# Up-projection of a gated MLP by seven block products in place of eight

## The chip, the cores and the metric

One core of a Trainium2 chip runs the whole program. The metric is the time of one execution on the device in microseconds; the time of a kernel is the median of its runs.

## What is computed

Two layers of a streaming encoder over 576 token columns (512 of one group, 64 of another, which share all weights). A layer has token mixers, cross-attention and a gated MLP with a causal convolution of width 3 between up-projection and activation; each has a norm before it and one behind it:

```python
def conv_ffn(h, w_up, conv_w, w_down, prev):
    u, state = causal_dwconv(h @ w_up, conv_w, prev)
    a, g = u[..., :D_FF], u[..., D_FF:]
    return (jax.nn.gelu(a, approximate=True) * g) @ w_down, state
...
    c = cross_attention(rmsnorm(x, g[2]), mem_k, mem_v, lp['w_ca_q'], lp['w_ca_o'])
    x = x + rmsnorm(c, g[3])
    f, ffn_state = conv_ffn(rmsnorm(x, g[4]), lp['w_up'], lp['ffn_conv_w'], lp['w_down'], hist['ffn'])
    x = x + rmsnorm(f, g[5])
```

Here `D_MODEL` is 1024 and `D_FF` 2816; all inputs and results are float32.

## The kernel before

Features lie on the 128 partitions, tokens on the columns, in two halves of 288 (`HALF`). Every float32 operand of a matmul is split (`split`, L129): ACT copies it to a rounded high part, DVE subtracts that from the source and has the low part. A product of two such operands is three matmuls (`mm3`, L152: lines 155 to 157). `load_w` (L137) has SP load 1024 weight columns and splits them in two pieces of 512, `wh` and `wl`, of which ten stand at a time.

The MLP is `ffn` (L1200). The 44 up-projection tiles go in 22 pairs, one tile of the gelu side and one of the gate side. A tile has eight k steps, so a pair has, in `emit`, 2 tiles x 2 token halves x 8 k steps x 3 matmuls. `scaled` (L317) takes each result out of PSUM on DVE and multiplies it by the norm `rn` on the way, for the split activations `h` in `boundary` (L320) are not yet divided by it. `done` runs the convolution (`conv_taps`, L942: one ACT operation and two DVE operations a tile, "taps" below), gelu, the product of the halves (DVE, L1226 and L1227) and the split into `ah` and `al`. After every four or five pairs (`STAGES`) `down` multiplies what is there by its part of the down-projection and adds it to `m` (DVE, L1269); `NACT` such activation tiles stand at a time. The last stage goes through `out_proj` (L333), which finishes the first token half (squares, mean, norm, addition to `x`) beside the matmuls of the second. The two pairs ahead of all others ("early tiles", `FEARLY`) run half 0 of both pairs before half 1, so that the boundary of half 1, from cross-attention, may still be at work.

The engines' orders come from a scheduler that reorders the program: weights of the next pair stand between a pair's evacuations and taps. Each engine then keeps its order. Results go to four PSUM banks (`DENSE`) in turn.

## Time and profile before

| | us |
|---|---|
| median of three runs | 2536.48 |
| lowest and highest | 2530.51, 2537.34 |
| the profiled execution | 2537.41 |
| its span in the profile | 2535.3 |
| PE, DVE, ACT, POOL busy | 2418.0, 1576.6, 1143.4, 403.6 |

Busy time is the union of an engine's instructions. On PE a matmul's row shows some 0.3 us, but matmuls overlap; count and stretch together give what one takes. The granted clock of a stretch is a share of 2.4 GHz, so 0.50 is 1.2 GHz. On a row of the timeline, the time in brackets is idle time ahead of the instruction and what ended it.

### The profile page before, as it was taken

To read this page: it belongs to the slowest core of one execution; us is meant where nothing else is said; L and a number is where in the kernel's file an instruction comes from. 1 tells how busy PE (TensorE), PEld (TensorE's weight loads), DVE (VectorE), ACT (ScalarE), POOL (GpSimd) and SP (SyncE) were. 2 spreads that over 40 slices of the span, in tenths; PEclk is the share of its full clock that TensorE was granted. 3 is DMA by queue.
4 is the path that set the end of the run, shared out by engine and by line. 5 is a ranking of instruction groups with operands and counts; after the bars stand their busy time and mean duration, and the time that the engine had idled before them with its cause. 6 is when DMAs were issued, how large, how long until landed. Compare 5 with 4: busy or idle time off the path is not lost. (4 is left out here: it accounts for less than half of the span.)

```text
span 2535.3 us, 45273 instructions
## 1 busy us (share of the span) xinstructions
PE 2418.0 (95%) x17478; PEld 2320.8 (92%) x17478; DVE 1576.6 (62%) x3249; ACT 1143.4 (45%) x2479; POOL 403.6 (16%) x723
## 2 busy tenths in 40 slices
PE   6999999999999999999989999999999899999997
PEld 6888897899998899999987889889999889999997
DVE  7757768644436675566676677774453767566565
ACT  4556545533345543333345554553233564433332
POOL 4000021002221421011130001100121323101012
PEclk9999999999998899999988999999999999999998
DMA  6763143333222032322233223323233202222321
GB/s 226 233 188 98 59 134 100 113 102 102 84 98 90 28 101 63 101 71 84 78 98 103 96 71 108 121 89 122 88 103 113 87 23 87 86 90 62 93 84 52
DMA packets 97510, 249.10 MB, mean 98 GB/s; under 512 B 12520, under 2 KB 26920, under 8 KB 97104
## 3 DMA queue, kind: packets, MB, share of 16 engines
q1 hardware_dynamic: 88880, 230.67, 29.4%
q0 software_dynamic: 3296, 8.54, 1.2%
q10 hardware_dynamic: 5120, 7.00, 0.8%
q8 instruction: 138, 2.26, 0.4%
q14 instruction: 76, 0.62, 0.1%
HBM read 206.18 MB, written 30.94 MB: 94 GB/s over the span
## 5 line engine op out<-in xcount | busy, mean ns | idle before, releaser
L123 ACT ACTIVATE wh<-raw 128x512 fp32r<-128x512 f32 (+2 forms) x674 | 405.1, 612 | 663.3 <-PE ps_S L156 300.9
L126 DVE TENSOR_TENSOR wl<-raw,wh 128x512 fp32r<-128x512 f32 (+2 forms) x674 | 444.7, 668 | 251.8 <-ACT wh L123 239.6
L155 PE MATMUL ps_d<-hh,wh 128*128 128x288 f32 (+1 forms) x1672 | 503.9, 301 | 0.8 <-DVE qbd L135 0.5
L157 PE MATMUL ps_d<-hh,wl 128*128 128x288 f32 (+1 forms) x1672 | 503.1, 301 | 0.0
L156 PE MATMUL ps_d<-hl,wh 128*128 128x288 f32 (+1 forms) x1672 | 502.1, 300 | 0.0
L156 PE MATMUL ps_S<-hl,wh 128*128 128x288 f32 (+1 forms) x1256 | 372.7, 297 | 0.4 <-DVE hl L285 0.4
L155 PE MATMUL ps_S<-hh,wh 128*128 128x288 f32 (+1 forms) x1256 | 371.7, 296 | 1.2 <-ACT hh L123 1.2
L157 PE MATMUL ps_S<-hh,wl 128*128 128x288 f32 (+1 forms) x1256 | 371.7, 296 | 0.0
L155 PEld LDWEIGHTS ps_d<-hh,wh 128*128 128x128 f32 (+1 forms) x1672 | 319.2, 191 | 3.3 <-issue 1.4
L157 PEld LDWEIGHTS ps_d<-hh,wl 128*128 128x128 f32 (+1 forms) x1672 | 319.0, 191 | 1.6 <-DVE wl L126 0.3
L156 PEld LDWEIGHTS ps_d<-hl,wh 128*128 128x128 f32 (+1 forms) x1672 | 319.2, 191 | 1.3 <-issue 0.2
L155 PEld LDWEIGHTS ps_S<-hh,wh 128*128 128x128 f32 (+1 forms) x1256 | 235.5, 188 | 2.8 <-ACT hh L123 1.8
L156 PEld LDWEIGHTS ps_S<-hl,wh 128*128 128x128 f32 (+1 forms) x1256 | 235.5, 187 | 1.5 <-DVE hl L285 0.6
L157 PEld LDWEIGHTS ps_S<-hh,wl 128*128 128x128 f32 (+1 forms) x1256 | 235.1, 187 | 0.6
L1086 POOL TENSOR_TENSOR mf<-mf,tm 128x288 f32<-128x288 f32 x64 | 64.4, 1006 | 451.4 <-DVE tm L1085 451.4
L955 POOL COPY fst<-u 128x2 f32<-128x2 f32 x88 | 32.2, 366 | 472.6 <-DVE u L319 472.6
L155 PE MATMUL ps_S<-ah,wh 128*128 128x288 f32 x352 | 105.6, 301 | 0.4 <-DVE m L1257 0.4
L156 PE MATMUL ps_S<-al,wh 128*128 128x288 f32 x352 | 105.8, 301 | 0.0
L157 PE MATMUL ps_S<-ah,wl 128*128 128x288 f32 x352 | 105.1, 299 | 0.0
L155 PE MATMUL ps_d<-ah,wh 128*128 128x288 f32 x352 | 104.0, 295 | 1.0 <-ACT ah L123 0.9
L157 PE MATMUL ps_d<-ah,wl 128*128 128x288 f32 x352 | 103.9, 295 | 0.0
L156 PE MATMUL ps_d<-al,wh 128*128 128x288 f32 x352 | 103.9, 295 | 0.0
(500 smaller groups left out, 5810.5 us busy)
## 6 DMA issues: line engine op xcount, KB each, us to landing
raw<-in_w_dram SPq DMA_DIRECT2D x250, 512.0 KB
raw<-in_down_dram SPq DMA_DIRECT2D x48, 256.0 KB
raw<-in_down_dram SPq DMA_DIRECT2D x32, 320.0 KB
of<-o_scr SPq DMA_DIRECT2D x24, 288.0 KB
x<-in_xT_dram SPq DMA_DIRECT2D x16, 288.0 KB
o_scr<-of SPq DMA_DIRECT2D x16, 288.0 KB
raw<-in_ukv_dram SPq DMA_DIRECT2D x8, 512.0 KB
kc_scr<-k SPq DMA_DIRECT2D x8, 512.0 KB
```

The lines of the kernel that those rows point to most:

```text
L123: self.nc.scalar.activation(out, in_, func, scale=scale, **k)
L126: self.nc.vector.tensor_tensor(out, a, b, op=ALU.subtract)
L155: mm(ps, w[0], x[0], start=first, stop=False)
L156: mm(ps, w[0], x[1], start=False, stop=False)
L157: mm(ps, w[1], x[0], start=False, stop=last)
L955: self.nc.gpsimd.tensor_copy(dst[:, 0:2], u[:, 512:514])
L1086: nc.gpsimd.tensor_tensor(mf[j][:, a:b], mf[j][:, a:b], tm[:, a:b], op=ALU.add)
```

## The change

Pairs 2 to 21 of the up-projection are computed by Strassen's scheme: the k range and the tokens are halved, and the two weight tiles of a pair, gelu side `a` and gate side `g`, are the two block rows. Seven products of four k steps, of sums of weights (`weights`, POOL) with sums of tokens (`token_sums`, once a layer), take the place of eight, and DVE adds up the results as it takes them out of PSUM (`pair`). The early pairs 0 and 1 stay as they are. So that tokens can be added, `boundary_n` divides `x` by its norm before the split; `x` itself goes to HBM and comes back at the last stage. POOL now has five sums of weights, one low part and the product of the halves (`done`) for each pair. There are six stages instead of five, ten activation tiles instead of 14, and six PSUM banks in the pairs.

```diff
-STAGES, NACT = ((0, 4), (4, 9), (9, 14), (14, 18), (18, 22)), 14
+STAGES, NACT = ((0, 4), (4, 8), (8, 12), (12, 16), (16, 20), (20, 22)), 10
 APOOL, XPOOL, OPOOL = (0, 1, 2, 3), (0, 1, 2, 3, 4), (0, 1, 2, 3, 4)
-DENSE, ATTN = ("d", "d", "S", "S"), ("d", "d", "n")
+DENSE, ATTN, SEVEN = ("d", "d", "S", "S"), ("d", "d", "n"), ("d", "d", "S", "S", "T", "T")
...
+    def boundary_n(self, xs, m, acc, hf, g1, g2, h, pool):
...
+        R = self.spread(self.rpow(self.mean_eps(acc)), "n", pool)
+        for kt in range(8):
+            t = pool.tile([P, 288], F32, tag="nt", name="nt", bufs=3)
+            nc.vector.scalar_tensor_tensor(t, m[kt][:, a:b], self.par(g1 + kt), R, op0=ALU.mult, op1=ALU.mult)
+            (nc.gpsimd if kt in APOOL else nc.vector).tensor_tensor(xs[kt][:, a:b], xs[kt][:, a:b], t, op=ALU.add)
+            nc.sync.dma_start(self.x_scr[kt, :, a:b], xs[kt][:, a:b])
+        self.x_rstd(xs, hf, pool)
+        for kt in range(8):
+            x = xs[kt][:, a:b]
+            nc.vector.scalar_tensor_tensor(x, x, self.par(g2 + kt), self.rn[:, a:b], op0=ALU.mult, op1=ALU.mult)
+            self.split(h[kt][0][:, a:b], h[kt][1][:, a:b], x)
...
         def emit(j, hf, W, us):
             a, b = HALF[hf]
-            e = min(b, 512)
             for k in range(2):
                 ps = self.dense_half(W[k], 0, 128, h, a, b)
-                self.scaled(us[k][:, a + 2:e + 2], ps[:, :e - a], a, e)
-                if b > 512:
-                    self.scaled(us[k][:, 516:580], ps[:, 512 - a:], 512, 576)
+                put(us[k], a, b, lambda o, c: self.act(o, ps[:, c]))
         def done(j, us):
...
-                y = pool.tile([P, 580], F32, tag="y", name="y", bufs=3)
+                y = self.xp.tile([P, 580], F32, tag="x", name="y")
...
-            t = pool.tile([P, NT], F32, tag="at", name="at", bufs=1)
-            nc.vector.tensor_tensor(t[:, 0:512], ys[0][:, 0:512], ys[1][:, 0:512], op=ALU.mult)
-            nc.vector.tensor_tensor(t[:, 512:], ys[0][:, 514:578], ys[1][:, 514:578], op=ALU.mult)
+            t = us[0]
+            nc.gpsimd.tensor_tensor(t[:, 0:512], ys[0][:, 0:512], ys[1][:, 0:512], op=ALU.mult)
+            nc.gpsimd.tensor_tensor(t[:, 512:576], ys[0][:, 514:578], ys[1][:, 514:578], op=ALU.mult)
...
+        def quad(src, eng=nc.vector):
+            hi = self.wp.tile([P, 512], F32R, tag="wh", name="wh")
+            lo = self.wp.tile([P, 512], F32R, tag="wl", name="wl")
+            self.act(hi, src)
+            eng.tensor_tensor(lo, src, hi.bitcast(F32), op=sub)
+            return hi, lo
...
+        def token_sums():
+            for kt in range(4):
+                b11, b12 = xs[kt][:, :288], xs[kt][:, 288:]
+                b21, b22 = xs[kt + 4][:, :288], xs[kt + 4][:, 288:]
+                nc.gpsimd.tensor_tensor(b11, b12, b11, op=sub)
+                part("t1", b11)
+                nc.gpsimd.tensor_tensor(b12, b22, b12, op=sub)
+                part("t3", b12)
+                nc.vector.tensor_tensor(b22, b22, b11, op=sub)
+                part("t2", b22)
+                nc.vector.tensor_tensor(b21, b21, b22, op=sub)
+            for kt in range(4):
+                t4 = (h[kt][0][:, 288:], h[kt][1][:, 288:])
+                self.split(t4[0], t4[1], xs[kt + 4][:, :288])
+                parts["t4"].append(t4)
+        def weights(j):
+            if j % 2:
+                ra = pool.tile([P, 1024], F32, tag="ra", name="ra", bufs=1)
+            else:
+                ra = self.bt.tile([P, 1152], F32, tag="pacc", name="ra", bufs=1)[:, 0:1024]
+            nc.sync.dma_start(ra, I["w8"][l, UP + 2 * j])
+            rg = self.raw.tile([P, 1024], F32, tag="raw", name="raw")
+            nc.sync.dma_start(rg, I["w8"][l, UP + 2 * j + 1])
+            a1, a2, g1, g2 = ra[:, :512], ra[:, 512:], rg[:, :512], rg[:, 512:]
+            tt = nc.gpsimd.tensor_tensor
+            w = {}
+            w["a11"] = quad(a1)
+            tt(g1, g1, g2, op=add)
+            tt(a1, g1, a1, op=sub)
+            w["s2"] = quad(a1)
+            w["a12"] = quad(a2)
+            tt(a2, a2, a1, op=sub)
+            tt(a1, g2, a1, op=sub)
+            w["s3"] = quad(a1)
+            w["s1"] = quad(g1)
+            w["a22"] = quad(g2)
+            w["s4"] = quad(a2, nc.gpsimd)
+            return w
         def pair(j):
+            us = padded(lambda: self.xp.tile([P, 580], F32, tag="x", name="u"), j)
+            w = weights(j)
+            lo, hi = slice(0, 288), slice(288, 576)
+            b11 = [(h[kt][0][:, lo], h[kt][1][:, lo]) for kt in range(4)]
+            b21 = [(h[kt][0][:, lo], h[kt][1][:, lo]) for kt in range(4, 8)]
+            b22 = [(h[kt][0][:, hi], h[kt][1][:, hi]) for kt in range(4, 8)]
+            def bank(q, b):
+                ps = self.dbank()[:, :288]
+                for kt in range(4):
+                    c = slice(128 * kt, 128 * kt + 128)
+                    self.mm3(ps, (q[0][:, c], q[1][:, c]), b[kt], kt == 0, kt == 3)
+                return ps
+            def temp(tag):
+                return self.bt.tile([P, 288], F32, tag=tag, name="u_" + tag, bufs=3)
+            tt = nc.vector.tensor_tensor
+            p1, u2, u3, u4 = temp("nt"), temp("sq"), temp("sq"), temp("nt")
+            self.act(p1, bank(w["a11"], b11))
+            tt(u2, bank(w["s2"], parts["t2"]), p1, op=add)
+            tt(us[0][:, 2:290], bank(w["a12"], b21), p1, op=add)
+            tt(u3, bank(w["s3"], parts["t3"]), u2, op=add)
+            ps5 = bank(w["s1"], parts["t1"])
+            put(us[1], 288, 576, lambda o, c: tt(o, ps5[:, c], u3[:, c], op=add))
+            tt(u4, ps5, u2, op=add)
+            tt(us[1][:, 2:290], bank(w["a22"], parts["t4"]), u3, op=add)
+            ps3 = bank(w["s4"], b22)
+            put(us[0], 288, 576, lambda o, c: tt(o, ps3[:, c], u4[:, c], op=add))
             done(j, us)
...
+                for kt in range(8):
+                    xs[kt] = self.xp.tile([P, NT], F32, tag="x", name="x")
+                    nc.sync.dma_start(xs[kt], self.x_scr[kt])
...
         for hf in range(2):
             for j, (us, W) in enumerate(pre):
                 emit(j, hf, W, us)
+        token_sums()
```

What the change moves in the engines' orders (names with their buffers' numbers):

Place 1, DVE in the middle of the pairs of layer 0, before: `y` are the taps, `wl` low parts of weights, `u` evacuations, `at` the product of the two halves, `al` the low part of an activation.

```order
L946 SCALAR_TENSOR_TENSOR y_11736<-u_11604,fprm_10410,y_11736 128x578
L126 TENSOR_TENSOR wl_12069<-raw_12066,wh_12068 128x512
L947 SCALAR_TENSOR_TENSOR y_11736<-u_11604,fprm_10410,y_11736 128x578
L319 TENSOR_TENSOR u_11605<-ps_d_11709,rn_10152 128x224
L319 TENSOR_TENSOR u_11605<-ps_d_11709,rn_10152 128x64
L126 TENSOR_TENSOR wl_12073<-raw_12066,wh_12072 128x512
L946 SCALAR_TENSOR_TENSOR y_11742<-u_11605,fprm_10410,y_11742 128x578
L947 SCALAR_TENSOR_TENSOR y_11742<-u_11605,fprm_10410,y_11742 128x578
L319 TENSOR_TENSOR u_11756<-ps_d_11782,rn_10152 128x288
L1226 TENSOR_TENSOR at_11749<-y_11736,y_11742 128x512
L1227 TENSOR_TENSOR at_11749<-y_11736,y_11742 128x64
L126 TENSOR_TENSOR al_11753<-at_11749,ah_11752 128x576
```

And after; `u_sq` and `u_nt` are evacuations of products that are added up:

```order
L1270 TENSOR_TENSOR wl_11929<-ra_11914,wh_11928 128x512
L963 SCALAR_TENSOR_TENSOR y_11727<-u_11580,fprm_10436,y_11727 128x578
L963 SCALAR_TENSOR_TENSOR y_11732<-u_11581,fprm_10436,y_11732 128x578
L964 SCALAR_TENSOR_TENSOR y_11727<-u_11580,fprm_10436,y_11727 128x578
L964 SCALAR_TENSOR_TENSOR y_11732<-u_11581,fprm_10436,y_11732 128x578
L1344 TENSOR_TENSOR u_sq_11787<-ps_T_11804,u_nt_11786 128x288
L1345 TENSOR_TENSOR u_11744<-ps_T_11818,u_nt_11786 128x288
L1270 TENSOR_TENSOR wl_11935<-ra_11914,wh_11934 128x512
L126 TENSOR_TENSOR al_11741<-u_11580,ah_11740 128x576
L1346 TENSOR_TENSOR u_sq_11788<-ps_d_11832,u_sq_11787 128x288
L1270 TENSOR_TENSOR wl_11939<-raw_11916,wh_11938 128x512
L1270 TENSOR_TENSOR wl_11943<-raw_11916,wh_11942 128x512
```

The product is gone to POOL, so between the last tap and `al` there are two evacuations and one low part; all four taps now stand together, with no evacuation between them.

Place 2, DVE behind the four early tiles of layer 0, before:

```order
L946 SCALAR_TENSOR_TENSOR y_10676<-u_10412,fprm_10410,y_10676 128x578
L126 TENSOR_TENSOR wl_10885<-raw_10882,wh_10884 128x512
L947 SCALAR_TENSOR_TENSOR y_10676<-u_10412,fprm_10410,y_10676 128x578
L319 TENSOR_TENSOR u_10413<-ps_S_10595,rn_10152 128x224
L319 TENSOR_TENSOR u_10413<-ps_S_10595,rn_10152 128x64
L126 TENSOR_TENSOR wl_10889<-raw_10882,wh_10888 128x512
L946 SCALAR_TENSOR_TENSOR y_10682<-u_10413,fprm_10410,y_10682 128x578
L319 TENSOR_TENSOR u_10438<-ps_S_10622,rn_10152 128x224
L319 TENSOR_TENSOR u_10438<-ps_S_10622,rn_10152 128x64
L947 SCALAR_TENSOR_TENSOR y_10682<-u_10413,fprm_10410,y_10682 128x578
```

And after; `tl` are low parts of token sums, and `wl_10837` is the first low part that the early pairs' successor, pair 2, needs and that does not stand further ahead:

```order
L964 SCALAR_TENSOR_TENSOR y_10774<-u_10438,fprm_10436,y_10774 128x578
L126 TENSOR_TENSOR tl_10757<-x_8449,th_10756 128x288
L963 SCALAR_TENSOR_TENSOR y_10779<-u_10439,fprm_10436,y_10779 128x578
L126 TENSOR_TENSOR tl_10762<-x_8457,th_10761 128x288
L964 SCALAR_TENSOR_TENSOR y_10779<-u_10439,fprm_10436,y_10779 128x578
L963 SCALAR_TENSOR_TENSOR y_10791<-u_10464,fprm_10436,y_10791 128x578
L963 SCALAR_TENSOR_TENSOR y_10796<-u_10465,fprm_10436,y_10796 128x578
L964 SCALAR_TENSOR_TENSOR y_10791<-u_10464,fprm_10436,y_10791 128x578
L126 TENSOR_TENSOR al_10788<-u_10438,ah_10787 128x576
L964 SCALAR_TENSOR_TENSOR y_10796<-u_10465,fprm_10436,y_10796 128x578
L1270 TENSOR_TENSOR wl_10837<-ra_10822,wh_10836 128x512
L1344 TENSOR_TENSOR u_sq_10859<-ps_S_10876,u_nt_10858 128x288
```

Low parts of weights stood among the taps and evacuations of the early pairs; now `wl_10837` stands behind the last token sum, the taps of both pairs and one `al`.

Place 3, PE ahead of the last down stage of layer 1, before (three more banks follow in the same way, nine matmuls each, ahead of the first that reads the last pair's `ah`):

```order
L155 MATMUL ps_d_29264<-ah_28521,wh_29260 128x288
L156 MATMUL ps_d_29264<-al_28522,wh_29260 128x288
L157 MATMUL ps_d_29264<-ah_28521,wl_29261 128x288
L155 MATMUL ps_d_29264<-ah_28945,wh_29260 128x288
L156 MATMUL ps_d_29264<-al_28946,wh_29260 128x288
L157 MATMUL ps_d_29264<-ah_28945,wl_29261 128x288
L155 MATMUL ps_d_29264<-ah_29097,wh_29260 128x288
L156 MATMUL ps_d_29264<-al_29098,wh_29260 128x288
L157 MATMUL ps_d_29264<-ah_29097,wl_29261 128x288
L155 MATMUL ps_S_29285<-ah_28521,wh_29281 128x288
```

And after; `ah_30054` is the last pair's:

```order
L156 MATMUL ps_d_30082<-al_29619,wh_30078 128x288
L157 MATMUL ps_d_30082<-ah_29618,wl_30079 128x288
L155 MATMUL ps_S_30097<-ah_29618,wh_30093 128x288
L156 MATMUL ps_S_30097<-al_29619,wh_30093 128x288
L157 MATMUL ps_S_30097<-ah_29618,wl_30094 128x288
L155 MATMUL ps_S_30114<-ah_29618,wh_30110 128x288
L156 MATMUL ps_S_30114<-al_29619,wh_30110 128x288
L157 MATMUL ps_S_30114<-ah_29618,wl_30111 128x288
L155 MATMUL ps_d_30131<-ah_29618,wh_30127 128x288
L156 MATMUL ps_d_30131<-al_29619,wh_30127 128x288
L157 MATMUL ps_d_30131<-ah_29618,wl_30128 128x288
L155 MATMUL ps_d_30082<-ah_30054,wh_30078 128x288
```

Ahead of the last pair's activation there were nine matmuls to each of four banks, and now there are three.

## Rows read from the trace of the kernel before

**Rows 1.** Busy times of the page: engine, us, share of the span, instructions.

```profile
PE 2418.0 (95%) x17478; PEld 2320.8 (92%) x17478; DVE 1576.6 (62%) x3249; ACT 1143.4 (45%) x2479; POOL 403.6 (16%) x723
```

**Rows 2.** Windows: stretch, its us, busy us (instructions) of each engine, PEclk, DMA share, GB/s.

```profile
865.00:877.00 12.00, 11.89 (x51) 11.32 (x52) 4.29 (x10) 3.84 (x9) 3.73 (x5) 0.50 0.21 57
...
900.00:1240.00 340.00, 340.00 (x2567) 340.00 (x2567) 208.99 (x405) 123.53 (x207) 45.74 (x146) 1.00 0.28 83
```

**Rows 3.** Groups by form, 900 to 1240 us: count, busy us, mean ns, idle before.

```profile
L126 DVE TENSOR_TENSOR wl<-raw,wh 128x512 fp32r<-128x512 f32 x104 | 70.8, 688 | 43.7 <-ACT wh L123 42.3
...
L947 DVE SCALAR_TENSOR_TENSOR y<-u,fprm,y 128x578 f32<-128x578 f32 x37 | 30.2, 817 | 0.5
...
L126 DVE TENSOR_TENSOR al<-at,ah 128x576 fp32r<-128x576 f32 x19 | 14.4, 756 | 9.9 <-ACT ah L123 9.8
```

**Rows 4.** Timeline of DVE in the MLP: start us, us, instruction.

```profile
902.08 0.51 DVE L319 TENSOR_TENSOR u<-ps_d,rn 128x224 f32<-128x224 f32 x2
902.52 0.81 DVE L946 SCALAR_TENSOR_TENSOR y<-u,fprm,y 128x578 f32<-128x578 f32 x1
...
905.38 0.44 DVE L319 TENSOR_TENSOR u<-ps_d,rn 128x288 f32<-128x288 f32 x1
905.74 0.81 DVE L947 SCALAR_TENSOR_TENSOR y<-u,fprm,y 128x578 f32<-128x578 f32 x1
906.47 0.68 DVE L126 TENSOR_TENSOR wl<-raw,wh 128x512 fp32r<-128x512 f32 x1
907.07 0.68 DVE L1226 TENSOR_TENSOR at<-y 128x512 f32<-128x512 f32 x1
...
908.80 0.75 DVE L126 TENSOR_TENSOR al<-at,ah 128x576 fp32r<-128x576 f32 x1
909.47 0.68 DVE L126 TENSOR_TENSOR wl<-raw,wh 128x512 fp32r<-128x512 f32 x1
```

**Rows 5.** Timelines of POOL and DVE in the merge of the mixers.

```profile
568.20 0.80 POOL L1086 TENSOR_TENSOR mf<-mf,tm 128x288 f32<-128x288 f32 x1 [6.56 <-DVE tm L1085]
569.85 1.28 POOL L1086 TENSOR_TENSOR mf<-mf,tm 128x288 f32<-128x288 f32 x1 [0.85 <-DVE tm L1085]
...
569.77 0.69 DVE L126 TENSOR_TENSOR wl<-raw,wh 128x512 fp32r<-128x512 f32 x1
```

**Rows 6.** POOL and DVE at the boundary; tile x: min, median, max ns.

```profile
882.91 0.90 POOL L243 TENSOR_TENSOR acc<-acc,sq 128x288 f32<-128x288 f32 x1 [0.38 <-ACT sq L123]
...
883.06 1.06 DVE L329 TENSOR_TENSOR x<-x,nt 128x288 f32<-128x288 f32 x1
...
L329 DVE TENSOR_TENSOR x<-x,nt x48: 442/448/1078, 750.1 to 2530.7; 128x288 f32<-128x288 f32 x48
```

**Rows 7.** Line 796, POOL operations of 576 columns: min, median, max ns.

```profile
L796 POOL TENSOR_TENSOR krf<-krf,cos x2: 1393/1406/1419, 90.9 to 1356.7; 32x576 f32<-32x576 f32 x2
```

**Rows 8.** Timelines of ACT and DVE at the boundary to the MLP, layer 0.

```profile
866.47 0.41 ACT L123 ACTIVATE rn<-ps_o 128x288 f32<-128x288 f32 x1 [2.15 <-PE ps_o L271]
...
875.40 1.36 DVE L328 SCALAR_TENSOR_TENSOR nt<-m,prm,ps_n 128x288 f32<-128x288 f32 x3 [0.41 <-PE ps_n L271]
...
886.81 0.50 DVE L285 SCALAR_TENSOR_TENSOR hl<-x,prm,hh 128x288 fp32r<-128x288 f32 x1
```

**Rows 9.** Timelines of DVE, ACT and PE ahead of the last down stage, layer 0.

```profile
1271.10 0.52 DVE L319 TENSOR_TENSOR u<-ps_d,rn 128x224 f32<-128x224 f32 x2
...
1275.87 0.68 ACT L123 ACTIVATE ah<-at 128x576 fp32r<-128x576 f32 x1 [2.61 <-DVE at L1227]
...
1276.61 0.40 PE L155 MATMUL ps_d<-ah,wh 128*128 128x288 f32 x1 [0.93 <-ACT ah L123]
```

More of the change, by code (lines that the diff above doesn't have):

```diff
@@ L333, in boundary @@
             self.x_rstd(xs, hf, pool)
+    def boundary_n(self, xs, m, acc, hf, g1, g2, h, pool):
+        nc = self.nc
+        a, b = HALF[hf]
+        R = self.spread(self.rpow(self.mean_eps(acc)), "n", pool)
[9 more added lines that the diff above has]
+            self.split(h[kt][0][:, a:b], h[kt][1][:, a:b], x)
     def out_proj(self, load, body, evac, m, finish, pool, skew=SKEW):
         nc = self.nc
-        accs = [self.sums(pool, "pacc") for _ in range(2)]
+        page = pool.tile([P, 1152], F32, tag="pacc", name="pacc", bufs=1)
+        accs = [[page[:, 288 * (2 * i + k):288 * (2 * i + k) + 288] for k in range(2)] for i in range(2)]
         ws = {}
@@ L1205, in ffn, with put @@
         acts = {}
+        add, sub = ALU.add, ALU.subtract
+        def put(us, a, b, f):
+            e = min(b, 512)
+            f(us[:, a + 2:e + 2], slice(0, e - a))
+            if b > 512:
+                f(us[:, 516:580], slice(512 - a, 576 - a))
         def emit(j, hf, W, us):
             a, b = HALF[hf]
-            e = min(b, 512)
             for k in range(2):
                 ps = self.dense_half(W[k], 0, 128, h, a, b)
-                self.scaled(us[k][:, a + 2:e + 2], ps[:, :e - a], a, e)
-                if b > 512:
-                    self.scaled(us[k][:, 516:580], ps[:, 512 - a:], 512, 576)
+                put(us[k], a, b, lambda o, c: self.act(o, ps[:, c]))
         def done(j, us):
@@ L1231, in done, with padded @@
             acts[j] = (hi, lo)
-        def start(j):
-            us = [pool.tile([P, 580], F32, tag="u", name="u", bufs=4) for _ in range(2)]
+        def padded(new, j):
+            us = [new() for _ in range(2)]
             for k in range(2):
-                self.pads(us[k], SF + 4 * (j + 22 * k))
-            W = [self.w8(l, UP + 2 * j + k) for k in range(2)]
-            return us, W
-        def pair(j):
-            us, W = start(j)
-            for hf in range(2):
-                emit(j, hf, W, us)
+                c = SF + 4 * (j + 22 * k)
+                self.act(us[k][:, 0:2], self.par(c, 2))
+                self.act(us[k][:, 514:516], self.par(c + 2, 2))
+            return us
@@ new lines, in quad, with part @@
+        def quad(src, eng=nc.vector):
[4 more added lines that the diff above has]
+            return hi, lo
+        def part(tag, src):
+            hi = pool.tile([P, 288], F32R, tag="t", name="th", bufs=24)
+            lo = pool.tile([P, 288], F32R, tag="t", name="tl", bufs=24)
+            self.split(hi, lo, src)
+            parts[tag].append((hi, lo))
@@ new lines, in ffn @@
+        parts = {k: [] for k in ("t1", "t2", "t3", "t4")}
+        def token_sums():
[13 more added lines that the diff above has]
+                parts["t4"].append(t4)
@@ L1269, in down @@
                         nc.vector.tensor_tensor(m[t][:, a:b], ps, m[t][:, a:b], op=ALU.add)
-        g = FEARLY
-        pre = [start(j) for j in range(g)]
+        pre = [(padded(lambda: pool.tile([P, 580], F32, tag="act", name="u", bufs=NACT), j),
+                [self.w8(l, UP + 2 * j + k) for k in range(2)]) for j in range(FEARLY)]
         for hf in range(2):
@@ L1275, in ffn @@
                 emit(j, hf, W, us)
+        token_sums()
         for j, (us, W) in enumerate(pre):
             done(j, us)
-        m.extend(pool.tile([P, 580], F32, tag="mf", name="m", bufs=8) for _ in range(8))
+        self.dtags = SEVEN
+        m.extend(pool.tile([P, NT], F32, tag="mf", name="m", bufs=8) for _ in range(8))
         todo = list(STAGES)
-        for j in range(g, 22):
+        for j in range(FEARLY, 22):
             pair(j)
```

8 lines of the change are left out of this document (5 added, 3 removed).

## The prediction

> **What bounds the kernel now.** I read the busy line of the page first, then the windows of the gated MLP, the groups of one MLP window, and the timelines of DVE and POOL there. The busy line [rows 1] shows PE at 95% of the span, DVE at 62%, POOL at 16%. The windows [rows 2] say where PE is the limit: from 900 to 1240 us, in the MLP of layer 0, PE is busy 340.00 of 340.00 us at full granted clock, so whatever takes matmuls away there shortens the span until another engine is in front. One 128x288 matmul costs 340.00 / 2567 = 0.1325 us of PE time; the 0.3 us of a single one on the timeline overlaps its neighbours. The groups and the DVE timeline [rows 3, 4] say who is next: DVE, with 208.99 us busy in the same window.
>
> **Matmuls removed.** A pair of up-projection tiles now takes 2 x 2 x 8 x 3 = 96 matmuls (12.72 us) and will take 7 x 4 x 3 = 84 (11.13 us). Pairs 2 to 21 of two layers: 40 x 12 = 480 matmuls, 480 x 0.1325 = **63.6 us off PE**. The order agrees: PE has 485 rows fewer.
>
> **DVE per pair.** From one start to the next [rows 4] a 512-column low part takes 0.60 us, a conv tap 0.73, the low part of an activation 0.67, a 288-column evacuation 0.37, one in two pieces (224 and 64) 0.44. Before: 4 x 0.60 + 4 x 0.73 + 0.67 + 2 x 0.37 + 2 x 0.44 + 0.74 for the product of the two halves (0.61 and 0.13, not all of it shown) = 8.35 us against 12.72 us of PE. After: 6 x 0.60 + 4 x 0.73 + 0.67 + 5 x 0.37 + 2 x 0.44 = 9.92 us against 11.13. On paper it still fits. ACT makes seven high parts in place of four and some small copies, about 8 us a pair, which PE's 11 us cover.
>
> **POOL per pair, and the place it shares.** POOL gets five sums of 512 columns, one low part and the activation product: seven of 512 and one of 64 columns. A 288-column POOL add alone takes 0.80 us [rows 5], one of 576 columns 1.39 to 1.42 [rows 7], so one of 512 takes about 0.80 + 224 x 0.59 / 288 = 1.26 us, and a pair about 9 us. But POOL and DVE do not run side by side. A POOL add beside a DVE low part, both with two SBUF inputs, took 1.28 us, 0.48 more [rows 5]. A DVE add that began 0.15 us into a POOL add took 1.06 us, against a median of 0.448 [rows 6]: it ended 0.31 us after POOL did. Each waits for the other's whole instruction. The first POOL add in rows 5 overlaps no such DVE work and pays nothing. The Trainium skill, GPSIMD Engine Reference, section 1 (Specifications), says that GpSimd's SBUF interfaces are shared with VectorE, with contention where the DVE instruction has two SBUF inputs; the trace agrees (1.28 against 0.80 us). By that rule the next term stands; if the two ran freely it would be nothing. In a pair, the two-input SBUF work of both is 7 x 1.1 + 0.3 of POOL (1.26 less the start of some 0.15) and about 6 x 0.5 + 4 x 0.65 + 0.6 of DVE, 14.2 us against PE's 11.13. Only the down stage after every four pairs (192 matmuls, 25.4 us) makes room: four pairs and a stage hold 4 x 14.2 + 8 x 0.5 = 61 us of it, against 4 x 11.13 + 25.4 = 70 us of PE.
>
> **What that costs.** In the four pairs ahead of a down stage DVE's own work is 4 x 9.92 = 39.7 us. By the order some 14 POOL operations of 512 columns fall there (the rest beside the down stage); DVE stands behind one for about half its time, 14 x 0.55 = 7.7 us. Per pair it waits some 1.6 us more at the low part of the activations (place 1 of the order): after the last tap come POOL's product (1.26 + 0.3) and ACT's high part (0.69, [rows 9]), 2.3 us and handing over, with 1.34 us of other DVE work between. That is 6.4 us. Sum 53.8 against PE's 44.5, so DVE comes out 9.3 us late. Six PSUM banks let PE run ahead by some five products of 12 x 0.1325 = 1.59 us, less what weights made late take of it; half of that lateness on PE would be 4.7 us. With the down stage (16 adds of 0.37, some ten low parts of 0.60 and twelve waits of 0.55: 18.5 us) a whole group takes DVE 72.3 us against PE's 69.9, 2.4 us more. I take **4 us for each of the eight full groups of four pairs, 32 us**. Bounds: 0 (all of it absorbed) to 12 (nothing absorbed, and DVE behind every POOL operation in full).
>
> **The way into the MLP.** Half 0 of the new boundary hides as before. It now needs the norm before the split, some 7 us of DVE, but the eight scaled low parts ahead of the adds are gone; before, the norm of half 0 was there at 866.47 us [rows 8], while PE ran at a granted 0.50, 1.2 GHz [rows 2]. For half 1 the same holds: nt begins at 875.40 and the last low part at 886.81 [rows 8]; I expect the last one near 892, and PE to end the four early tiles near 898, where it does now. Then DVE has the token sums: 24 operations of about 0.40 us with two taps among them, and POOL's eight subtractions in their way, 13 us; behind them four taps and an activation's low part, 6 us, before the first low part that PE lacks (place 2 of the order). That is about 911 us, where PE could use it at 898 + 3.2: 10 us idle. The pair's chain of POOL sum, ACT, DVE adds 3, pairs 3 and 4, which no down stage helps, 2 each; and such idle time has been followed by the lower clock (51 matmuls in 12 us instead of some 90 [rows 2]), for which I take 2. **19 us a layer, 38 in all.** Bounds 8 and 30 a layer.
>
> **The end of a layer.** Now 36 matmuls stand ahead of the first that needs the last activation (4.8 us); it comes 1275.87 - 1271.10 + 0.68 = 5.45 us after the last evacuation began, and PE idles 0.93 us [rows 9]. After: 12 matmuls, 1.6 us (place 3 of the order), and a longer chain: evacuation 0.5, ACT 0.8, four taps 3.0, POOL's product 1.6, ACT 0.7, some 6.8 with handing over. Idle 5.2, 4.3 more. The last stage is half as long (6.4 us a token half), so the first half's norm, eight nt and four adds, hides less well: 3 us; lower clock 1.7. **9 us a layer, 18 in all**; bounds 4 and 15 a layer.
>
> The x tiles go out by 16 more DMAs and come back by eight a layer, at 0.3 to 0.4 us of issue on SP, which is mostly free; they land beside the last stage's matmuls and the first mean: 0, or 3 us a layer if the last four land late, within that term's bounds. The extra down stage's 16 adds a layer fall where DVE has room: 0, or 6 us a layer if it hasn't, within the group's bounds.
>
> **Sum.** The profiled execution took 2537.4 us, 0.9 over the median of the three runs shown (2536.48). 2537.4 - 63.6 + 32 + 38 + 18 = 2561.8; against the median, **2561 us**, 1% slower.
>
> **Rivals.** (B) *POOL sets the pace.* DVE's order stands still behind each POOL sum, so the four pairs take 12 us more each group: 8 x 12 = 96 in place of 32, **2625 us**. For it: 14.2 us of shared time a pair against 11.13; against it: the order brings POOL's sums forward into the down stage. (C) *The banks absorb it.* No group term, ends as costed: 2561 - 32 = **2529 us**, where the seven products pay for their own ends. (D) *Faster.* DVE's lateness never passes the six banks, and the token sums finish while PE is still in the early tiles: 2536.5 - 63.6 + 2 x 10 + 2 x 5 = **2503 us**. It decides itself at the point where DVE's time for a pair, waits and its part of the down stage included, stays under PE's 69.9 / 4 = 17.5 us: my sum has 72.3 / 4 = 18.1, of which 5.2 are waits, so an eighth less waiting would do. For it: DVE had 131 us free in the 340 us window. That the change doesn't do what it says is ruled out by the order's count of matmuls.
>
> **How the numbers follow.** About 0.3%, 7.6 us, is what a measurement of this kernel tells from no change. Forecast 0.45, B 0.18, C 0.17, D 0.18, anything else 0.02. Slower: B and nearly all of the forecast, 0.60. Within 0.3%: most of C and a little of the forecast, 0.12. Faster: D and the rest of C, 0.28. The range 2502 to 2626 reaches from D to B, with about half of each outside. The forecast's own range is 2535 to 2595.
>
> **What would show it.** In the profile after: PE busy near 480 x 0.1325 = 64 us less, yet new idle PE time of 10 us or more behind the first early tiles of each layer, ended by DVE low parts; idle of about 5 us at the last down stage, ended by the activation's high part; POOL operations of 512 columns that average over 1.5 us, not 1.26; DVE taps and low parts with means well above 0.82 and 0.69 us [rows 3]; and PE under 98% busy in windows over the pairs. If POOL's 512-column operations stay at 1.3 us and the MLP window still shows PE 100% busy, my group term is wrong and D or C holds. If PE goes on with the pairs without a gap after the early tiles, the term of 38 us is wrong.

## The result, and the profile after

The changed kernel takes **2672.86 us** (median of 4 runs, 2668.07 to 2678.12) against 2536.91 for the kernel before: a ratio of 1.054, 95% interval 1.0511 to 1.057. Slower was right; the size was not: +136 us where +24 was forecast, and outside the range. The profiled execution has a span of 2676.3 us at a mean granted clock of 0.953 (0.979 before). Its busy line answers to [rows 1]:

```profile
PE 2429.3 (91%) x16998; PEld 2307.7 (86%) x16998; DVE 1776.3 (66%) x3433; ACT 1246.3 (47%) x2943; POOL 688.6 (26%) x675
```

PE has the 480 matmuls less, and is busy 11 us longer all the same: the idle gaps below are followed by stretches at a lower clock. No engine but PE is above 66%, so no engine is full; in the groups below DVE has 77%.

The windows of layer 0's MLP say where the time went (columns as in [rows 2]). The first four are of the changed kernel, from the last mean ahead of the MLP to the mean at its end; the first of them is the beginning of the second:

```profile
884.00:898.60 14.60, 10.06 (x42) 7.74 (x42) 11.81 (x18) 6.68 (x24) 8.62 (x9) 0.66 0.03 12
...
884.00:998.60 114.60, 95.44 (x629) 90.87 (x629) 75.75 (x132) 58.63 (x154) 50.81 (x42) 0.88 0.18 57
998.60:1336.00 337.40, 299.68 (x2124) 291.70 (x2123) 259.71 (x429) 140.08 (x325) 136.16 (x106) 0.96 0.24 74
1336.00:1365.80 29.80, 16.52 (x105) 15.61 (x103) 20.50 (x41) 16.90 (x37) 13.84 (x16) 0.82 0.46 161
```

The kernel before has PE at 100% from 886.66 on, and then this end:

```profile
886.66:900.00 13.34, 13.34 (x103) 13.04 (x104) 9.70 (x22) 7.80 (x13) 2.67 (x7) 1.00 0.39 118
...
1240.00:1302.30 62.30, 56.24 (x411) 54.98 (x409) 42.52 (x83) 28.21 (x53) 16.39 (x30) 0.96 0.27 81
```

Each stretch less its matmuls at 0.1325 us is what it loses. The way in: 114.6 - 629 x 0.1325 = 31 us, of which 14.6 - 42 x 0.1325 = 9 are lost before 898.60, at the boundary of half 1. The four full groups of four pairs and a down stage: 337.4 - 2124 x 0.1325 = 56, 14 a group. The end: 29.8 - 13.9 = 15.9, of which the kernel before already loses 62.3 - 54.5 = 7.8. Together 95 us a layer, less 31.8 for the matmuls.

Not all of that is idle time. PE is busy 95.44, 299.68 and 16.52 us in the three parts, where their matmuls at 0.1325 take 83.3, 281.4 and 13.9: some 33 us are matmuls that took longer, in windows with mean granted clocks of 0.88, 0.96 and 0.82, and with the first one behind each gap (0.61 us at 1141.43). The end of the kernel before has 1.8 of this. Of the 14 us a group, 9.4 are idle and 4.6 are slower matmuls.

**Inside a group** two things show. First a chain. Timelines of DVE, POOL, ACT and PE in one pair, with the taps of the next (start us, us, instruction, idle before and what ended it):

```profile
1102.52 0.68 DVE L1270 TENSOR_TENSOR wl<-ra,wh 128x512 fp32r<-128x512 f32 x1
...
1103.28 1.29 POOL L1312 TENSOR_TENSOR ra<-raw,ra 128x512 f32<-128x512 f32 x1 [2.62 <-DVE wl L1270]
...
1105.27 1.29 DVE L1270 TENSOR_TENSOR wl<-ra,wh 128x512 fp32r<-128x512 f32 x2 [1.27 <-ACT wh L123]
1106.48 2.57 DVE L963 SCALAR_TENSOR_TENSOR y<-u,fprm,y 128x578 f32<-128x578 f32 x2
1108.97 2.56 DVE L964 SCALAR_TENSOR_TENSOR y<-u,fprm,y 128x578 f32<-128x578 f32 x2
1111.45 0.45 DVE L1344 TENSOR_TENSOR u_sq<-ps_d,u_nt 128x288 f32<-128x288 f32 x1
...
1121.54 1.58 DVE L963 SCALAR_TENSOR_TENSOR y<-u,fprm,y 128x578 f32<-128x578 f32 x2 [0.91 <-ACT y L123]
1123.04 1.55 DVE L964 SCALAR_TENSOR_TENSOR y<-u,fprm,y 128x578 f32<-128x578 f32 x2
...
1106.70 1.72 POOL L1315 TENSOR_TENSOR ra<-ra 128x512 f32<-128x512 f32 x1 [2.14 <-DVE wl L1270]
1108.51 1.68 POOL L1316 TENSOR_TENSOR ra<-raw,ra 128x512 f32<-128x512 f32 x1
...
1110.21 0.63 ACT L123 ACTIVATE wh<-ra 128x512 fp32r<-128x512 f32 x1 [2.36 <-POOL ra L1316]
...
1111.95 0.40 PE L155 MATMUL ps_d<-hh,wh 128*128 128x288 f32 x1 [2.19 <-DVE u_sq L1344]
```

Read it from hand to hand. L1312 makes s2 in the place of a11, so POOL waits until DVE has a11's low part. Then ACT makes the high part, DVE the low part, and only when DVE is through with the places can POOL write s4's and s3's sums there; ACT waits for those. All engines take turns. Secondly, the four taps beside the two sums take 5.0 us from 1106.48 on, where the next pair's four, with no sum beside them, take 3.0 from 1121.54 on, and the evacuation that PE needs (L1344) stands behind them in DVE's order.

The second place is ahead of each down stage: the same timelines, with m, the evacuation of the stage, behind the taps:

```profile
1134.93 2.59 DVE L963 SCALAR_TENSOR_TENSOR y<-u,fprm,y 128x578 f32<-128x578 f32 x2
1137.44 3.56 DVE L964 SCALAR_TENSOR_TENSOR y<-u,fprm,y 128x578 f32<-128x578 f32 x2
1140.93 0.81 DVE L1383 TENSOR_TENSOR m<-ps_S,m 128x288 f32<-128x288 f32 x2
...
1135.24 1.66 POOL L1311 TENSOR_TENSOR raw<-raw 128x512 f32<-128x512 f32 x1 [8.47 <-DVE wl L1270]
1136.98 1.66 POOL L1312 TENSOR_TENSOR ra<-raw,ra 128x512 f32<-128x512 f32 x1
1138.60 1.78 POOL L1311 TENSOR_TENSOR raw<-raw 128x512 f32<-128x512 f32 x1
...
1141.43 0.61 PE L155 MATMUL ps_S<-ah,wh 128*128 128x288 f32 x1 [4.61 <-DVE m L1383]
```

Both show in the groups of the page and of the views by form (count, busy us, mean ns, idle before), which answer to [rows 3]:

```profile
L1270 DVE TENSOR_TENSOR wl<-ra,wh 128x512 fp32r<-128x512 f32 x160 | 131.7, 828 | 137.9 <-ACT wh L123 137.6
L963 DVE SCALAR_TENSOR_TENSOR y<-u,fprm,y 128x578 f32<-128x578 f32 x88 | 101.2, 1183 | 10.2 <-ACT y L123 10.1
...
L1251 POOL TENSOR_TENSOR u<-y 128x512 f32<-128x512 f32 x44 | 65.8, 1496 | 172.5 <-DVE y L964 100.3 <-ACT y L123 63.5 <-DVE u_sq L1344 8.7
L1316 POOL TENSOR_TENSOR ra<-raw,ra 128x512 f32<-128x512 f32 x40 | 58.4, 1461 | 3.0
L1315 POOL TENSOR_TENSOR ra<-ra 128x512 f32<-128x512 f32 x40 | 55.0, 1376 | 89.8 <-DVE wl L1270 89.8
...
L123 ACT ACTIVATE wh<-ra 128x512 fp32r<-128x512 f32 x200 | 120.1, 624 | 257.9 <-POOL ra L1316 119.4 <-POOL ra L1312 92.8 <-PE ps_T L157 11.3
```

DVE waits 137.9 us for ACT ahead of these low parts, ACT 212 us for POOL's sums, POOL 89.8 us for DVE ahead of one of them alone. In the four groups of layer 0 DVE is idle 337.4 - 259.7 = 77.7 us, 19.4 a group; its two longest waits there (us in total, times, longest):

```profile
DVE wl L1270 <- ACT wh L123: 43.8, 18, 4.3
DVE al L126 <- ACT ah L123: 15.0, 16, 2.2
```

**At the ends** PE waits where the forecast put it: behind the early tiles, at the last down stage, at the mean behind it (the last line is the same mean in the kernel before):

```profile
917.50 0.61 PE L157 MATMUL ps_S<-hh,wl 128*128 128x288 f32 x1 [6.63 <-DVE wl L1270]
...
922.55 0.61 PE L155 MATMUL ps_T<-th,wh 128*128 128x288 f32 x1 [2.29 <-ACT wh L123]
...
1342.04 0.61 PE L155 MATMUL ps_d<-ah,wh 128*128 128x288 f32 x1 [5.33 <-ACT ah L123]
...
1365.75 0.77 PE L255 MATMUL ps_T<-ones,acc 128*96 128x1 f32 x4 [7.42 <-DVE acc L243]
...
1302.29 0.80 PE L255 MATMUL ps_T<-ones,acc 128*96 128x1 f32 x4 [4.48 <-DVE acc L243]
```

### The profile page after: what moved, and what is told of

Read it like the earlier page. It is cut to its first block, busy times and chain, and to the rows that moved or that the text cites. A ratio compares the mean times of both kernels' runs of the same rounds, so it can differ in the third digit from the quotient of the medians.

```text
span 2676.3 us, 45260 instructions
## 1 busy us (share of the span) xinstructions
PE 2429.3 (91%) x16998; PEld 2307.7 (86%) x16998; DVE 1776.3 (66%) x3433; ACT 1246.3 (47%) x2943; POOL 688.6 (26%) x675
## 5 line engine op out<-in xcount | busy, mean ns | idle before, releaser
L123 ACT ACTIVATE wh<-raw 128x512 fp32r<-128x512 f32 (+3 forms) x578 | 350.8, 617 | 355.9 <-PE ps_d L156 147.2
L126 DVE TENSOR_TENSOR wl<-raw,wh 128x512 fp32r<-128x512 f32 (+3 forms) x498 | 341.5, 693 | 166.8 <-ACT wh L123 155.2
L155 PE MATMUL ps_d<-hh,wh 128*128 128x288 f32 x1236 | 380.7, 308 | 9.7 <-DVE u_sq L1344 4.4
L157 PE MATMUL ps_d<-hh,wl 128*128 128x288 f32 x1236 | 378.6, 306 | 6.8 <-DVE wl L1270 6.8
L156 PE MATMUL ps_d<-hl,wh 128*128 128x288 f32 x1236 | 378.7, 306 | 5.8 <-DVE hl L126 5.8
L155 PEld LDWEIGHTS ps_d<-hh,wh 128*128 128x128 f32 x1236 | 240.5, 195 | 16.0 <-DVE u_sq L1344 4.8
L156 PE MATMUL ps_S<-hl,wh 128*128 128x288 f32 (+1 forms) x840 | 251.1, 299 | 1.1 <-DVE hl L285 1.0
L156 PEld LDWEIGHTS ps_d<-hl,wh 128*128 128x128 f32 x1236 | 240.1, 194 | 10.0 <-DVE hl L126 8.1
L157 PEld LDWEIGHTS ps_d<-hh,wl 128*128 128x128 f32 x1236 | 240.6, 195 | 8.8 <-DVE wl L1270 7.2
L1270 DVE TENSOR_TENSOR wl<-ra,wh 128x512 fp32r<-128x512 f32 x160 | 131.7, 828 | 137.9 <-ACT wh L123 137.6
```

The costliest lines, as they stand in the source:

```text
L123: self.nc.scalar.activation(out, in_, func, scale=scale, **k)
L126: self.nc.vector.tensor_tensor(out, a, b, op=ALU.subtract)
L155: mm(ps, w[0], x[0], start=first, stop=False)
L156: mm(ps, w[0], x[1], start=False, stop=False)
L157: mm(ps, w[1], x[0], start=False, stop=last)
L1270: eng.tensor_tensor(lo, src, hi.bitcast(F32), op=sub)
```

## The experiments

Three theories. **L**: POOL and DVE exclude each other, and DVE stands behind whole POOL operations. **C**: the chain of sums through shared places is too long for engines that run in order. **E**: the ends lose the time. An edit also moves other instructions, since a scheduler sets each engine's order, so differences below some 10 us are not read closely.

**1. Sums left out.**

```diff
-            tt(g1, g1, g2, op=add)
-            tt(a1, g1, a1, op=sub)
...
-            tt(a2, a2, a1, op=sub)
-            tt(a1, g2, a1, op=sub)
```

> The four weight sums of each pair are left out: the seven products read the weight quarters unsummed, so the result differs, while the matmuls, the high and low parts and the evacuations are those of the changed kernel. POOL keeps two of its six 512-column operations a pair. Theory L (DVE and POOL exclude each other, and DVE stands behind whole POOL operations): a group of four pairs and a down stage falls from 84 us to 72 to 76, so 2575 to 2600 us, and DVE's taps and low parts come back to means near 0.85 and 0.65 us. Theory C (the chain POOL sum, ACT, DVE is too long and the engines run in order; the exclusion matters little): also faster, since the chain is cut, 2590 to 2630, with taps still over 1.1 us. Theory E (the lost time is in the two ends of each MLP, not in the pairs): 2650 to 2675.

Measured 2525.71 us, ratio 0.9952 (0.9933 to 0.9971). The four sums cost 147 us, more than either theory gave. The pairs then run without a gap; the window of this run:

```profile
935.00:1255.00 320.00, 320.00 (x2412) 319.90 (x2411) 253.56 (x462) 162.56 (x372) 60.60 (x53) 1.00 0.29 89
```

**2. A copy for each sum.**

```diff
-            tt(g1, g1, g2, op=add)
-            tt(a1, g1, a1, op=sub)
+            cp = nc.gpsimd.tensor_copy
+            cp(g1, g2)
+            cp(a1, g1)
```

(and so for the other two)

> Each of the four weight sums on POOL becomes a POOL copy of the same 512 columns into the same place (one SBUF input in place of two), so the result differs, but every step of the chain and the order of all engines stay. Theory L: if an operation with one input does not exclude DVE, the time comes near that of the run without the sums, 2575 to 2610 us, and the copies keep one duration whether DVE works or not. Theory C: the chain is as long as before, so no change, 2655 to 2680. Theory E: 2655 to 2680.

Measured 2577.02 us, 96 less than with the sums, as L has it. But a copy alone takes about half of a sum, so the chain was cut as well.

**3. Sums on DVE.**

```diff
-            tt = nc.gpsimd.tensor_tensor
+            tt = nc.vector.tensor_tensor
```

> The four weight sums of each pair run on DVE in place of POOL; the result is the reference's. DVE gets 4 x 0.6 = 2.4 us more a pair, about 10 a group, and stands behind two POOL operations a pair, not six. Theory L: a group comes to 75 to 79 us, 2600 to 2635. Theory C: DVE has more to do in the same order and the chain has the same length, 2670 to 2720. Theory E: 2655 to 2690.

Measured 2580.86 us, 92 less, though DVE has 10 us more to do a group: below all that was expected. C, as DVE's load, falls here; a chain that changes engines less often does not. The edit does three things at once: a sum no longer changes engines, no longer stands beside DVE's work, and takes some 0.7 us instead of some 1.4.

**4. Eight products, all else of the change kept.**

```diff
         def pair(j):
...
-            w = weights(j)
...
+            W = [self.w8(l, UP + 2 * j + k) for k in range(2)]
+            for hf in range(2):
+                emit(j, hf, W, us)
             done(j, us)
```

> The pairs compute eight products again (two dense halves a tile, as the kernel before), with everything else of the change kept: the new boundary, the token sums (which now only cost time and spoil four tiles of h, so the result differs), six down stages, the product of the two halves on POOL. It prices the two ends and the stages. Forecast's terms: 2537 + 38 + 18 = 2593. If the ends cost what they seem to in the trace after (86 us): 2615 to 2630. Theory E: 2630 to 2675, that is nearly all of the change's loss without one of the seven products.

Measured 2569.98 us, ratio 1.015 (1.0111 to 1.019): the boundary, the token sums, the stages and the product on POOL cost 32 us by the medians (28 to 48 by the interval of the ratio), less than the forecast's 56 and not nearly all. E falls. In this run's trace PE is 100% busy in the pairs, and waits at the end as in the changed kernel (view of PE's timeline, layer 0):

```profile
920.00:1280.00 360.00, 360.00 (x2720) 360.00 (x2718) 180.40 (x273) 162.30 (x427) 32.78 (x38) 1.00 0.27 83
...
912.54 0.40 PE L157 MATMUL ps_S<-hh,wl 128*128 128x288 f32 x1 [1.10 <-DVE wl L126]
...
1291.80 0.61 PE L155 MATMUL ps_d<-ah,wh 128*128 128x288 f32 x1 [4.72 <-ACT ah L123]
```

Behind the early tiles it waits 1.10 us, not 6.63 + 2.29: that wait belongs to the seven products, not to the token sums alone. The run keeps the boundary of half 1 and the end of a layer; the 9 and 8 us that these lose in the changed kernel, 34 in two layers, are about what it costs.

**5. Each copy twice**, so that the chain is as long as with sums.

```diff
-            tt(g1, g1, g2, op=add)
-            tt(a1, g1, a1, op=sub)
+            def cp(o, i):
+                nc.gpsimd.tensor_copy(o, i)
+                nc.gpsimd.tensor_copy(o, i)
...
+            cp(g1, g2)
+            cp(a1, g1)
```

> As the run with copies in place of the four weight sums (result differs), but each copy is made twice in a row, since one copy took only 0.69 to 0.77 us and so had cut the chain as well. Now a step of the chain takes about 1.4 us, no less than a sum alone (1.27). Theory L (exclusion): POOL is busy as long as in the changed kernel but DVE does not stand behind it, 2575 to 2605 us, taps still near 0.93 us. Theory C (long chain): back to 2640 to 2675.

Measured 2624.08 us, between the two: 49 less than with the sums, 47 more than with single copies. The 47 are the longer chain, or the second copy's own time beside DVE: this run's trace shows that a copy is not free of DVE. A group's timelines, and the durations of one line's copies (min/median/max ns):

```profile
1094.04 1.02 POOL L1313 COPY ra<-ra 128x512 f32<-128x512 f32 x1
1095.13 1.02 POOL L1312 COPY ra<-raw 128x512 f32<-128x512 f32 x1
...
1093.44 1.16 DVE L963 SCALAR_TENSOR_TENSOR y<-u,fprm,y 128x578 f32<-128x578 f32 x1
1094.51 2.25 DVE L964 SCALAR_TENSOR_TENSOR y<-u,fprm,y 128x578 f32<-128x578 f32 x2
...
L1312 POOL COPY ra<-raw x80: 611/617/1150, 881.9 to 2556.3; 128x512 f32<-128x512 f32 x80
```

Medians over all 512-column copies: 0.617 us with no two-input DVE work beside them, 1.02 beside it. Two copies are no shorter a step than a sum (1.23 us against 1.29, both alone), so the 49 us are put down to DVE's shorter standing behind each. As the copies exclude DVE too, that is not the whole price of the exclusion.

**6. Taps of the pair ahead of a stage written behind it.**

```diff
-            done(j, us)
+            return us
...
-            pair(j)
+            us = pair(j)
             if todo and j == todo[0][1]:
                 down(*todo.pop(0))
+            done(j, us)
```

> The conv taps, the product and the split of the pair that stands just ahead of a down stage are written behind that stage, so that DVE's evacuations of the stage no longer stand behind its four taps; the result is the reference's. In the trace after, PE idles 3.6 to 5.1 us at this place in each full group. If that idle is an order of its own (in-order DVE): 8 x 4.5 = 36 us less, 2630 to 2645. If DVE is simply that much late over the group (theory L, the lateness shows wherever PE next needs it): the idle moves elsewhere and 0 to 15 us are gained, 2658 to 2673.

Measured 2658.07 us: 15 less of the 36 that the gap would be worth. Most of the lateness moves on.

**7. Pair 2 by eight products**, ahead of the token sums.

```diff
+        u2 = padded(lambda: pool.tile([P, 580], F32, tag="act", name="u", bufs=NACT), FEARLY)
+        W2 = [self.w8(l, UP + 2 * FEARLY + k) for k in range(2)]
+        for hf in range(2):
+            emit(FEARLY, hf, W2, u2)
         token_sums()
...
+        done(FEARLY, u2)
...
-        for j in range(FEARLY, 22):
+        for j in range(FEARLY + 1, 22):
```

> Pair 2 of each layer computes eight products, written ahead of the token sums, so PE has 12.7 us of matmuls while DVE and POOL make the sums; the result is the reference's. It adds 12 matmuls a layer, 3.2 us in all. In the trace after, PE idles 6.6 + 2.3 us behind the early tiles, with a lower granted clock up to 930 us. If the token sums cost what the forecast said (10 us idle and 2 of clock of the 19 a layer): 2673 + 3 - 24 = 2652, range 2645 to 2660. If DVE's lateness moves on to the next pair: 2668 to 2680.

Measured 2646.42 us: 26 less, as expected for a wait behind the early tiles that PE's own work can fill, 13 us a layer.

**8. Edits 3 and 7 with a longer last stage** (`(16, 19), (19, 22)` in STAGES).

> Three edits together, the result is the reference's: the four weight sums on DVE (2581 us alone), pair 2 by eight products, and a last down stage of three activations in place of two (the one before it of three). Theory L with the ends as the traces show them: 2581 + 3 - 2 x (8.5 + 4) - 2 x 3 = 2553, range 2540 to 2562. If DVE, which now carries the sums, is the bound over a group: 2565 to 2585.

Measured 2550.45 us, ratio 1.0057 (1.004 to 1.0075), as expected.

**9. The second sum in a place of its own.**

```diff
-            tt(a1, g1, a1, op=sub)
+            q2 = self.wp.tile([P, 512], F32, tag="wl", name="q2")
+            tt(q2, g1, a1, op=sub)
...
-            tt(a2, a2, a1, op=sub)
-            tt(a1, g2, a1, op=sub)
+            tt(a2, a2, q2, op=sub)
+            tt(a1, g2, q2, op=sub)
```

(s2 is then split from q2)

> The second weight sum goes to a tile of its own (a slot of the low parts' pool) in place of overwriting its source; so POOL need not wait for DVE's low part of a11 before it, nor for that of s2 before the third sum. Work, engines and sizes stay; the result is the reference's. The runs so far: copies made twice 2624, sums left out 2526, changed kernel 2673. If the chain through the shared places (sum, high part, low part, next sum) is what costs about two thirds of that: 2615 to 2650. If the length of the POOL operations and the exclusion alone count: 2662 to 2682.

Measured 2635.38 us: 37 us came from the places alone, with the same work on the same engines. The groups of this run show what took over:

```profile
L1270 DVE TENSOR_TENSOR wl<-q,wh 128x512 fp32r<-128x512 f32 x40 | 43.7, 1092 | 17.4 <-ACT wh L123 11.9 <-PE ps_S L157 5.5
...
L1316 POOL TENSOR_TENSOR ra<-ra,q 128x512 f32<-128x512 f32 x40 | 62.9, 1573 | 73.2 <-DVE wl L1270 73.2
```

DVE's idle time ahead of its low parts from the sums is down to 17.4 + 22.8 us from 137.9, but the operations themselves are longer: these 160 low parts have a mean of 0.94 us instead of 0.83, and the sum for s4, now L1316, 1.57 instead of 1.38. Without the turns they collide.

**10 to 12. The combination with a last stage of four** (stages of 4, 4, 4, 3, 3, 4); in 11 edit 6 too; in 12 the product of a12, which needs no sum, ahead of that of s2:

```diff
             w["a11"] = quad(a1)
+            w["a12"] = quad(a2)
...
-            w["a12"] = quad(a2)
...
+            tt(us[0][:, 2:290], bank(w["a12"], b21), p1, op=add)
             tt(u2, bank(w["s2"], parts["t2"]), p1, op=add)
-            tt(us[0][:, 2:290], bank(w["a12"], b21), p1, op=add)
```

> The combination (sums on DVE, pair 2 by eight products; 2550 us) with stages of 4, 4, 4, 3, 3, 4 activations, so the last one has 36 matmuls ahead of the first that needs the last activation, as in the kernel before. In the combination's trace PE idles 5.5 us there and 6.2 us at the last mean. If the short last stage makes these: 2 x (4.5 + 1.5) = 12 less, 2533 to 2543. If the longer chain of the last pair makes them whatever the stage: 2547 to 2553.

> As e10 with the taps of the pair ahead of a stage written behind the stage. Alone this edit gave 15 us with the sums on POOL. With the sums on DVE PE idles only some 2.7 us a group, 1.2 of it at this place: 0 to 8 us less than e10, 2527 to 2541; more if DVE's delay there also lowers the clock.

> As e10, with the product of a12, which needs no sum, second in place of third, so the first two sums have one more product (1.6 us of matmuls) of time before PE needs s2. If the chain of sums still holds PE up in the pairs (the trace of the combination shows 1.4 us idle a group ahead of a product with th, that is s2's or s3's): 1.4 x 8 = 11 less than e10, 2522 to 2535. If not: the same as e10 within 5.

Measured 2544.48, 2552.1 and 2543.42 us. The longer last stage gave at most 6 of the 12, and PE still idles 6 us ahead of it (12's row below); the late taps, of which up to 8 us had been expected, and the order of products gave nothing that can be told.

**13 to 15.** 13 puts a down stage between the last pair's products and its taps (stages of 4, 4, 4, 3, 2, 2, 3). 14 also moves the product of the two halves and s4's low part to DVE, so that POOL has no work in the pairs. 15 is the changed kernel with 9's place and 12's order of products.

```diff
-            nc.gpsimd.tensor_tensor(t[:, 0:512], ys[0][:, 0:512], ys[1][:, 0:512], op=ALU.mult)
+            nc.vector.tensor_tensor(t[:, 0:512], ys[0][:, 0:512], ys[1][:, 0:512], op=ALU.mult)
...
-            w["s4"] = quad(a2, nc.gpsimd)
+            w["s4"] = quad(a2)
```

> As e12 (2543 us) with stages of 4, 4, 4, 3, 2, 2, 3 activations, of which the sixth is written behind the last pair's products and ahead of its taps, so PE has 96 matmuls (12.7 us) while DVE, ACT and POOL make the last activation; one stage more costs DVE 16 adds a layer. If the last pair's chain makes the 6.0 us idle at the last stage: 2 x (6 + 1) = 14 less and 2 x 1 for the added stage, 2528 to 2535. If DVE is what is late there (it now has a stage's evacuations in the same place): 2538 to 2546.

> As e13 with the product of the two halves and the low part of s4 on DVE too, so POOL has no work in the pairs. DVE gets 4 x (0.74 + 0.6) = 5.4 us more a group, on some 67 busy of 75. If the exclusion by the two POOL operations that are left still costs as much as that: 2525 to 2540. If DVE becomes the bound: 2545 to 2575.

> The changed kernel with the second sum in a place of its own (2635 us alone) and the product of a12, which needs no sum, second in place of third; all sums stay on POOL, the result is the reference's. If the chain of sums is what is left of the cost ahead of th products: 2575 to 2610. If the exclusion and DVE's lateness ahead of the down stage (3.6 to 6.8 us idle a group in e9) make the rest: 2622 to 2640.

Measured 2556.26, 2532.9 and 2619.93 us. In 13 the wait ahead of the last stage goes (PE's timeline of 12, then of 13), but PE waits 4.58 us in the last pair's products instead:

```profile
1269.66 0.85 PE L155 MATMUL ps_S<-ah,wh 128*128 128x288 f32 x2 [5.98 <-ACT ah L123]
```

```profile
1257.93 0.61 PE L155 MATMUL ps_T<-th,wh 128*128 128x288 f32 x1 [4.58 <-ACT wh L123]
...
1280.21 0.37 PE L155 MATMUL ps_S<-ah,wh 128*128 128x288 f32 x1 [1.27 <-DVE m L1383]
```

So a stage's matmuls in between do cover the last pair's chain, but the edit lost 13 us, which neither expectation had; what of that is the added stage was not taken apart. 14 against 13: the product and the low part on POOL still cost 23 us. 15: more slack in the chain gives 53 us and leaves 2620.

**16 to 18. Nothing on POOL in the pairs.** 16 is 12 with 14's move; 17 is the changed kernel with the sums, the low part and the product on DVE and nothing else; 18 is 16 with stages of 4, 4, 4, 4, 3, 3.

> As e12 (sums on DVE, pair 2 by eight products, a12 second, last stage of four; 2543 us) with the product of the two halves and the low part of s4 on DVE too. If the exclusion gives what it gave between e13 and e14: 2543 - 23 = 2520, range 2512 to 2530, which is below the kernel before. If the stage in between made e13 so sensitive: 2530 to 2545.

> The changed kernel with one edit: the four sums, the low part of s4 and the product of the two halves of each pair on DVE; POOL has no work in the pairs. With the sums alone moved it was 2581. DVE gets 5.4 us more a group. If two POOL operations a pair still exclude DVE at a price: 2550 to 2572. If DVE becomes the bound, 2580 to 2605.

> As e16 with a last stage of three (4, 4, 4, 4, 3, 3). e10 gave 6 us for the last stage of four against three: 3 to 8 us more than e16. If the end does not hang on the stage: the same as e16 within 3.

Measured **2517.37** us for 16, ratio 0.9927 (0.9906 to 0.9949), faster than both kernels; 2552.8 for 17; 2518.01 for 18, so here the end does not hang on the length of the last stage (3 to 8 us more had been expected if it did). 17 shows it in one edit: 120 of the 136 us go away when POOL leaves the pairs. A window over the pairs and a group of run 16:

```profile
1000.00:1250.00 250.00, 249.95 (x1881) 249.36 (x1880) 237.51 (x477) 125.00 (x290) 0.61 (x1) 1.00 0.28 89
```

```profile
L1270 DVE TENSOR_TENSOR wl<-ra,wh 128x512 fp32r<-128x512 f32 x190 | 127.8, 683 | 11.5 <-ACT wh L123 10.2
L963 DVE SCALAR_TENSOR_TENSOR y<-u,fprm,y 128x578 f32<-128x578 f32 x88 | 68.9, 816 | 1.9 <-ACT y L123 1.9
```

DVE does everything, is busy 95% of the window, and PE still has no gap.

## Why the prediction was wrong

**Matmuls removed**: right, 480 fewer. But PE's busy time rose by 11 us where it was to fall by 64, so 75 us went into slower matmuls, of which the windows of layer 0 hold 31 (33 less the 1.8 of before). The forecast had 2 + 1.7 us a layer for the lower clock, all at the ends, and none in the groups.

**The end of a layer** (9 us a layer, idle 5.2 at the last stage): right, 5.33 us idle and some 8 us a layer in the windows.

**The way into the MLP** (19 us a layer, bounds 8 to 30): measured 31, just outside. The wait behind the early tiles was right, 6.63 + 2.29 us where 10 was forecast, and from 898.60 on the way in loses 22 in all. The other 9 are the boundary of half 1, which was put at nothing ("For half 1 the same holds"): up to 898.60 PE does 42 matmuls in 14.6 us at a granted clock of 0.66, and the wait behind the early tiles begins at 910.87, not near 898. Run 7 fills the wait behind the early tiles with one pair's matmuls.

**What that costs**, the group term, is the step that failed: 4 us a group, bounds 0 to 12, where the trace has 14. Of the 95 us a layer it carries 40 of the 51 that were missed.

The load was right. DVE's own work and its standing behind POOL came to 39.7 + 5.9 + 6.0 + 14 x 0.55 + 12 x 0.55 = 65.9 us a group in the forecast's sum; DVE is busy 259.7 / 4 = 64.9. The exclusion in it was rather too large. The lengthening of taps and low parts over that of run 16, where POOL is out, is 88 x (1.183 - 0.816) + 88 x (1.073 - 0.813) + 160 x (0.828 - 0.683) + 80 x (0.992 - 0.682) = 103 us in 40 pairs (1.073 and 0.992: the second taps and the low parts from raw), 10.3 us a group; the sum had 14.3. It had counted five sums on POOL, as the section on the change says, where the code has four, and POOL's 512-column operations came to means of 1.32 to 1.50 us, not over 1.5.

The waits were wrong. The sum had 6.4 us of them a group, all ahead of the activations' low part; DVE is idle 19.4. Ahead of the activations' low part it is 15.0 / 4 = 3.8; 43.8 / 4 = 11 are ahead of the low parts of L1270, for ACT, where the sum had nothing. Three of the four sums overwrite a place that DVE must first have read, so a pair is a chain of turns between POOL, ACT and DVE. The prediction priced that chain at 7 us a layer, on the way in (3, 2 and 2 for the first pairs), and at nothing in the groups. It set 72.3 us of DVE's work and waits against PE's 69.9, as if each engine had only to be less loaded than PE; in run 16 DVE is busy 95% of the window and PE loses nothing. Run 9 shows the chain by itself: another place for one sum gives 37 us with the work and the engines kept.

How the 147 us of the sums divide is not settled. Loosening the chain gave 37 (9) and with the order of products 53 (15); shorter operations beside DVE gave 49 (5). These are what each edit gave, not shares: where the turns are loosened the operations overlap and lengthen each other, and that a sum takes longer on POOL than on DVE was not tested alone. The remaining 45 are open.

Rival B, POOL setting the pace at 2625 us, came nearest, by luck: it had 12 us a group, but POOL is busy 136.2 of the 337.4 us of the groups, and DVE stood behind it less than the forecast had, not more. The reason held against it, that the order brings sums forward into the down stage, does not help: the trace after shows them there too (1135 to 1140 us), where they delay the stage's evacuations behind the taps. Rival D, that a little less waiting makes the change pay (2503 us), has its condition in run 16: DVE is not late in the pairs, and the time is 2517 us. But that took POOL out of the pairs and other edits at the ends.
